# A batched weight gradient with Strassen pairs: two more pairs, another visit order, and banks that start from other products

## The chip, the cores and the metric

The kernel runs on one core of a Trainium2 chip. The metric is the device time of one execution in microseconds. A profile of one execution gives the time of each instruction; its span, from the first to the last instruction, is 1.5 to 1.8 us shorter than the device time.

## The reference

```python
batch, m, k, n = 16, 512, 1024, 768
grad_weight = np.einsum('bmk,bmn->kn', input, grad_output)   # float32
```

With the batch folded into the rows this is one product: X is 8192 x 1024, G is 8192 x 768, and the output X^T G is 1024 x 768 in float32. The contraction runs over 8192 rows, 64 slices of 128.

## The kernel before

**Slices, pairs, quarters.** The 64 slices are loaded as 32 items of two slices. The output is cut in four blocks: A (left half of the columns of X, left half of those of G), B (left, right), C (right, left) and D (right, right), each 512 x 384, that is four quarters of 128 rows. A matmul takes 128 columns of X as weights and 384 columns of G as moving operand. An item of the kind `s` in `LOADS` stays two single slices, each of which adds to A, B, C and D: 16 matmuls a slice, 32 for the two. An item of the kind `P` is a Strassen pair: its two slices are treated as the second index of a 2 x 2 block product, so seven products do the work of eight: 28 matmuls. Two of the seven go straight to A and D; the others are collected in five sums of their own, m, n, o, p and q, and are added to the blocks they belong to once at the end.

**The presums.** A pair needs sums and differences of its bf16 halves. VectorE makes them in six instructions, `sum_g1`, `sum_g2`, `sum_g3` (lines 130, 134, 139), `sum_x1`, `sum_x2`, `sum_x3` (lines 144, 148, 153). Then m = (x2)(g2), n = (x1)(raw g), o = (raw x)(g3), p = (raw x)(g3), q = (x1)(raw g), D takes x3 and g1, A takes x3 and g1.

**Banks.** PSUM has eight banks here, two groups of four (one bank for a quarter). So only two products are open at a time. `ORDER` is a list of visits. `A14:2` brings product A up to its item 14; a figure after the colon says how many of the four banks ScalarE drains (the last ones); a part after `!` closes the product, and its four figures say how many VectorE presums or shares are put in the queue ahead of the drain of each quarter; a figure in front of the letter puts presums ahead of the visit. An engine does its own list in order. A bank that VectorE drains is added to the running sum in SBUF (line 295, or 293 where it is the first). A bank that ScalarE drains has first been filled with the running sum by ScalarE (line 267), so that the matmuls add on to it, and is copied out at the end (line 291). Another product can open a group only when the one before has been drained from its banks.

**Shares.** At the end `SHARES` lists the additions of m to q to the blocks: `t1`, `t2`, `t3` for the upper rows, `l1`, `l2`, `l3` for the lower, each for four quarters. `t1`, `t2`, `l1`, `l2` are 768 columns wide and serve two blocks in one instruction (line 162); `t3` (line 173) and `l3` (line 184) subtract from one block, 384 columns.

**Loads and stores.** The first slice comes in float32 by the queues of SyncE and ScalarE and is rounded by VectorE and ScalarE (`round_by`, line 202). The others are issued by GpSimd and rounded to bf16 on the way, one slice at a time (lines 110 and 112), from item `MERGED` on two slices together (lines 105 and 106). Fourteen items can be held; a load waits for a free buffer. The output is stored by SyncE a quarter at a time, in program order (line 299). The last quarter of the last visit is split in 256 and 128 columns, with a store for each (lines 327 to 336), where the last visit also opens its product.

Of the kernel before, what the change touches and what calls it, by code (L numbers as in the profile page):

```python
# [1 line left out]

# [5 lines left out]

P = 128

LOADS = "ssssssssPPPPPPPPPPPPPPPPPPPPPsss"

ORDER = (
    "A1:4 C1:2!0,0,0,0 D1:2 A2!0,0,0,0 D2 B3:4 D3 D4!0,0,0,0 B4 C4:2 C5 B5 C6!0,0,0,0 B6 A6:2 B7 "
    "A8!0,0,0,0 D8:2 B8 B9 D10!0,0,0,0 B10 B11 C7:2 C9 B12 C11 B13!0,0,0,0 C12 C13 A14:2 C14 "
    "C16!0,0,0,0 A15 B16:2!3,0,0,0 D16:2 3A17!3,0,0,1 n2:4!0,1,1,0 D17 D18 m2:4!3,0,1,0 "
    "q3:4!1,1,1,1 D19 o1:4 o2 o3 1o4!2,1,0,0 D20!0,0,0,0 p4:4 n3:3 3p5!3,0,0,0 n4 A21:2!3,0,0,1 "
    "n6 1m6:4!3,1,0,1 n7 o7:2!2,0,0,1 q7:2!2,0,0,2 n8 p8:2!2,0,0,1 D24:2!1,1,0,2 n9 A25:3!3,0,1,1 "  # L20
    "n10 o10:2!2,0,0,1 m10:2 2n11!2,0,0,1 m11 q11:2!2,0,1,1 p12:2!1,1,0,2 D28:2 m12 3D29!3,0,0,0 "
    "m13 A28:2 2m14!1,0,0,0 A30 o12:2 o13 3o15!3,0,0,1 A31 q15:2!2,1,0,2 A32!0,0,0,0 n16:2 "
    "D32:4!6,1,1,1 p17:2 1n18!3,0,0,0 p18 m17:2 2p19!3,0,0,0 m19 D35:3!3,1,0,2 o20:2 m20 "
    "3o21!2,0,0,0 m21!0,0,0,0 q20:2 p20:4 p21!4,1,0,0 q21!0,0,0,0 D39:0 n21:4!3,1,0,1 D41 "
    "A37:4!2,1,1,1 D42 B17:0 D43!6,0,0,0 B19 B22!0,0,0,0 C19:0 C22!0,0,0,0 A43:0!4,0,0,0 "
).split()


SHARES = (
    "t10 t11 t12 t13 l20 t20 t21 t22 t23 l21 l22 l23 l10 l11 l12 l13 l30 l31 l32 l33 t30 t31 t32 "  # L30
    "t33 "
).split()

WARMUP = [512] * 10 + [128] * 2
PAIRS_HELD = 14
SUMS_HELD = 9

MERGED = 7


@with_exitstack
def kernel(
# [6 lines left out]
    nc = tc.nc  # L49
# [4 lines left out]
    _, _, N = grad_output.shape  # L54
    S = B * M // P
    KH = K // 2
    NH = N // 2
    Q = KH // P
# [3 lines left out]
    OUT = out.rearrange("(ks p) n -> p ks n", p=P)  # L62
# [7 lines left out]
    acc = accp.tile([P, 2 * Q, N], f32, name="acc")  # L70

    macc = accp.tile([P, 5, Q, NH], f32, name="macc")
    SLOT = {"n": 0, "p": 1, "m": 2, "o": 3, "q": 4}
# [23 lines left out]
    items = []  # L97
# [56 lines left out]

    def settled(row, q):
        for p, (_, banks) in opened.items():
            assert p not in ("CD" if row else "AB") or not banks[q][1]

    def share(row, slots, q):
        settled(row, q)  # L160
        dst = acc[:, row + q, :].rearrange("p (h n) -> p h n", h=2)
        nc.vector.tensor_add(out=dst, in0=dst, in1=macc[:, slots, q, :])  # L162

    def top1(q):
        share(0, slice(2, 4), q)

    def top2(q):
        share(0, slice(1, 5, 3), q)

    def top3(q):  # L170
        settled(0, q)
        c = acc[:, q, 0:NH]
        nc.vector.tensor_sub(out=c, in0=c, in1=macc[:, 4, q, :])  # L173

    def low1(q):
        share(Q, slice(0, 3, 2), q)

    def low2(q):
        share(Q, slice(1, 4, 2), q)

    def low3(q):
        settled(Q, q)
        c = acc[:, Q + q, NH:N]
        nc.vector.tensor_sub(out=c, in0=c, in1=macc[:, 0, q, :])

    filler = []
    for i, item in enumerate(items):
        if item[0] == "P":
            filler += [(f, i) for f in (sum_g1, sum_g2, sum_g3, sum_x1, sum_x2, sum_x3)]
    share_by = {"t1": top1, "t2": top2, "t3": top3, "l1": low1, "l2": low2, "l3": low3}  # L190
    filler += [(share_by[c[:2]], int(c[2:])) for c in SHARES]
    filler.reverse()

    def fill(n):
# [20 lines left out]
    streams = {  # L215
        p: [i for i, item in enumerate(items) if item[0] in KINDS.get(p, "P")] for p in "ABCDmnopq"
    }

    LAST_PAIR = max([i for i, item in enumerate(items) if item[0] == "P"], default=0)

    def operands(p, i, q):
        kind, x, g = items[i]
# [16 lines left out]
    def sum_of(p, q):  # L239
        if p in SLOT:  # L240
            return macc[:, SLOT[p], q, :]
        row = q if p in "AB" else Q + q
        return acc[:, row, 0:NH] if p in "AC" else acc[:, row, NH:N]
# [3 lines left out]
    slots = [0, 1]  # L247
    used = set()

    def visit(p, upto, byact, close, ahead, last):  # L250
        items_now = streams[p][done[p] : upto]
        done[p] = upto
        opening = p not in opened
        if opening:

            tail = p in "ABCD" and streams[p][upto - len(items_now)] > LAST_PAIR - 2
            slot = slots.pop(0)
            banks = []
            for q in range(Q):
                name = f"bank{slot * Q + q}"  # L260
                bank = psum.tile([P, 512], f32, name=name)[:, 0:NH]
                act = q >= Q - byact
                carried = act and not fresh[p]
                assert not (carried and tail)
                if carried:
                    assert name in used
                    nc.scalar.copy(out=bank, in_=sum_of(p, q))  # L267
                used.add(name)
                banks.append((bank, carried, act))
            opened[p] = (slot, banks)  # L270
        slot, banks = opened[p]
        final = upto == len(streams[p])

        def mm(q, j):
            stat, mov = operands(p, items_now[j], q)
            bank, carried, _ = banks[q]
            nc.tensor.matmul(  # L277
                bank,
                stat,
                mov,  # L280
                start=opening and j == 0 and not carried,
                stop=close and j == len(items_now) - 1,
                skip_group_check=carried,
            )

        def shut(q):
            fill(ahead[q])
            bank, _, act = banks[q]
            dst = sum_of(p, q)
            if act:  # L290
                nc.scalar.copy(out=dst, in_=bank)  # L291
            elif fresh[p]:
                nc.vector.tensor_copy(out=dst, in_=bank)  # L293
            else:
                nc.vector.tensor_add(out=dst, in0=bank, in1=dst)  # L295
            if final and p in "ABCD":
                row = q if p in "AB" else Q + q
                c0 = 0 if p in "AC" else NH
                nc.sync.dma_start(out=OUT[:, row, c0 : c0 + NH], in_=dst)

        if len(items_now) == 1:
            for q in range(Q):
                mm(q, 0)
            if close:
                for q in range(Q):
                    shut(q)
        else:
            for q in range(Q):
                if last and q == Q - 1 and opening:
                    break  # L310
                for j in range(len(items_now)):
                    mm(q, j)
                if close:
                    shut(q)
            else:
                q = None
            if q is not None:

                fill(ahead[q])
                dst = sum_of(p, q)  # L320
                row = q if p in "AB" else Q + q
                b0 = 0 if p in "AC" else NH
                for c0, c1, name in ((0, 256, None), (256, NH, f"bank{slots[0] * Q}")):
                    bank = banks[q][0] if name is None else psum.tile([P, 512], f32, name=name)
                    for j in range(len(items_now)):
                        stat, mov = operands(p, items_now[j], q)
                        nc.tensor.matmul(
                            bank[:, 0 : c1 - c0],
                            stat,
                            mov[:, c0:c1],  # L330
                            start=j == 0,
                            stop=j == len(items_now) - 1,
                        )
                    d = dst[:, c0:c1]
                    nc.vector.tensor_add(out=d, in0=bank[:, 0 : c1 - c0], in1=d)  # L335
                    nc.sync.dma_start(out=OUT[:, row, b0 + c0 : b0 + c1], in_=d)
        if close:
            fresh[p] = False
            del opened[p]
            slots.append(slot)  # L340

    for n, step in enumerate(ORDER):
        step, _, ahead = step.partition("!")
        step, _, byact = step.partition(":")
        at = next(c for c in step if c.isalpha())
        before, upto = step.split(at)
        if n == 1:
            round_by("DVE", g0, gf, NH, N)
        if n == 2:
            round_by("DVE", x1, xf[1], 4 * P, 6 * P)  # L350
            round_by("ACT", x1, xf[1], 6 * P, 8 * P)
            round_by("DVE", x1, xf[1], 0, 2 * P)
            round_by("ACT", x1, xf[1], 2 * P, 4 * P)
        fill(int(before or 0))
        ahead = [int(a) for a in ahead.split(",")] if ahead else None
        visit(at, int(upto), int(byact or 0), ahead is not None, ahead, n == len(ORDER) - 1)
    assert not filler and not opened


# [28 lines left out]
```

## Time and profile before

| what | value |
|---|---|
| device time, median of three | 166.4 us (166.32 to 166.52) |
| profiled span | 164.9 us |
| TensorE busy, matmuls | 158.8 us, 958 (12 of them a warm-up) |
| VectorE busy, instructions | 114.3 us, 231 |
| ScalarE busy, instructions | 83.1 us, 196 |
| read from HBM, written | 58.72 MB, 3.15 MB |

A share of busy time is a mean over the whole span. What matters for a change of the order is which engine the others wait for in each stretch, which the chain of waits shows. Matmuls overlap: the duration of one, 328 ns, is about twice the step from one start to the next. The loads keep the DMA engines busy to about 141 us, as the page's slices show:

```profile
DMA  5999999999999999999999999999999999300875
```

The three columns after that are without a transfer, and the last belong to the stores.

### The profile page before, as it was taken

What the parts mean: (1) busy time and instruction counts of PE and PEld (TensorE: products, weight loads), DVE (VectorE), ACT (ScalarE), POOL (GpSimd) and SP (SyncE); (2) the same over time, 40 slices, a digit from 0 to 9 for tenths busy, and PEclk for the clock granted to TensorE, in tenths of its full rate; (3) what the DMA queues carried; (4) which work ended last, traced back from release to release, by engine and by line L of the source; (5) the groups of instructions that cost most, each with busy time, mean ns of one, the idle gap of its engine ahead of it and who ended that gap; (6) DMA issues with size and microseconds to landing.
All of it is one profiled execution on the core that took longest, in us unless ns stands there. A gap on an engine that the chain in (4) does not pass through costs nothing.

```text
span 164.9 us, 2645 instructions
## 1 busy us (share of the span) xinstructions
PE 158.8 (96%) x958; PEld 93.8 (57%) x958; DVE 114.3 (69%) x231; ACT 83.1 (50%) x196; POOL 39.9 (24%) x79
## 2 busy tenths in 40 slices
PE   8999999999999999999999999999999999999991
PEld 2456556566545656555566566545656566566560
DVE  0602222002969678879997997998858979999992
ACT  3554442150726586875766744357645568970000
POOL 7444535432222222222222222222122000000000
PEclk9999999999999999999999999999999999999998
DMA  5999999999999999999999999999999999300875
GB/s 179 294 207 208 209 207 210 208 218 209 220 209 216 213 209 218 211 208 221 208 212 213 213 213 214 213 210 215 213 216 212 215 211 214 75 0 0 288 284 191
DMA packets 13836, 33.39 MB, mean 203 GB/s; under 512 B 1536, under 2 KB 5632, under 8 KB 13824
## 3 DMA queue, kind: packets, MB, share of 16 engines
q0 software_dynamic: 10800, 28.64, 89.0%
q1 hardware_dynamic: 2736, 3.54, 6.2%
q10 hardware_dynamic: 288, 1.05, 1.6%
q8 instruction: 7, 0.11, 0.3%
q14 instruction: 5, 0.04, 0.1%
HBM read 58.72 MB, written 3.15 MB: 375 GB/s over the span
## 4 chain that ended last, share of the span: by engine, by line
PE 91%; DVE 6%; issue 1%; DVEq 0%
PE bank L277 88%; PE bank L88 3%; DVE acc L295 3%; DVE xe L144 1%; DVE acc L293 1%; DVE macc L295 1%; DVE acc L173 0%; DVE xp L153 0%; DVE acc L335 0%; DVE xe L148 0%; DVEq L383 0%
## 5 line engine op out<-in xcount | busy, mean ns | idle before, releaser
L277 PEld LDWEIGHTS <-xp 128*128 128x128 bf16 x682 | 66.7, 98 | 46.1 <-issue 1.3
L277 PE MATMUL bank<-gp,xp 128*128 128x384 bf16 x514 | 88.4, 328 | 0.3 <-DVE acc L293 0.2
L291 ACT COPY macc<-bank 128x384 f32<-128x384 f32 x63 | 27.5, 488 | 26.8 <-PE bank L277 26.6
L295 DVE TENSOR_TENSOR acc<-bank,acc 128x384 f32<-128x384 f32 x39 | 19.9, 553 | 28.0 <-PE bank L277 27.7
L291 ACT COPY acc<-bank 128x384 f32<-128x384 f32 x48 | 21.3, 485 | 35.7 <-PE bank L277 35.2
L277 PEld LDWEIGHTS <-xe 128*128 128x128 bf16 x252 | 24.4, 98 | 17.4 <-DVE xe L144 1.5
L277 PE MATMUL bank<-ge,xp 128*128 128x384 bf16 x168 | 31.1, 327 | 0.7 <-DVE xp L153 0.7
L277 PE MATMUL bank<-gp,xe 128*128 128x384 bf16 x168 | 30.4, 327 | 0.6 <-DVE xe L144 0.6
L106 POOL DMA_DIRECT2D xp<-in_input_dram x25 | 13.2, 527 | 41.8 <-DMA xp<-in_input_dram 24.3
L105 POOL DMA_DIRECT2D gp<-in_grad_output_dram x25 | 13.2, 527 | 31.8 <-DMA gp<-in_grad_output_dram 11.4
L295 DVE TENSOR_TENSOR macc<-bank,macc 128x384 f32<-128x384 f32 x29 | 15.2, 554 | 6.6 <-PE bank L277 6.3
L267 ACT COPY bank<-macc 128x384 f32<-128x384 f32 x43 | 19.2, 505 | 0.0
L267 ACT COPY bank<-acc 128x384 f32<-128x384 f32 x36 | 16.1, 497 | 0.0
L144 DVE TENSOR_TENSOR xe<-xp 128x1024 bf16<-128x1024 bf16 x21 | 14.4, 685 | 1.9 <-DMA xp<-in_input_dram 1.9
L277 PE MATMUL bank<-ge,xe 128*128 128x384 bf16 x84 | 15.5, 327 | 0.0
L153 DVE TENSOR_TENSOR xp<-xp 128x1024 bf16<-128x1024 bf16 x21 | 14.4, 685 | 0.0
L162 DVE TENSOR_TENSOR acc<-acc,macc 128x768 f32<-128x768 f32 x16 | 14.1, 953 | 0.0
L130 DVE TENSOR_TENSOR ge<-gp 128x768 bf16<-128x768 bf16 x21 | 11.6, 552 | 0.8 <-DMA gp<-in_grad_output_dram 0.8
L139 DVE TENSOR_TENSOR gp<-gp 128x768 bf16<-128x768 bf16 x21 | 11.6, 552 | 0.0
L148 DVE TENSOR_TENSOR xe<-xp 128x512 bf16<-128x512 bf16 x21 | 8.8, 419 | 0.0
L112 POOL DMA_DIRECT2D xp<-in_input_dram x12 | 6.5, 538 | 9.0 <-DMA xp<-in_input_dram 6.8
L110 POOL DMA_DIRECT2D gp<-in_grad_output_dram x13 | 7.1, 549 | 3.8 <-DMA gp<-in_grad_output_dram 3.1
(18 smaller groups left out, 27.6 us busy)
## 6 DMA issues: line engine op xcount, KB each, us to landing
xp<-in_input_dram POOLq DMA_DIRECT2D x25, 512.0 KB, 16.9
gp<-in_grad_output_dram POOLq DMA_DIRECT2D x25, 384.0 KB, 16.7
xp<-in_input_dram POOLq DMA_DIRECT2D x12, 256.0 KB, 8.5
out_dram<-acc SPq DMA_DIRECT2D x15, 192.0 KB, 2.1
gp<-in_grad_output_dram POOLq DMA_DIRECT2D x13, 192.0 KB, 8.5
xf<-in_input_dram ACTq DMA_DIRECT2D x2, 512.0 KB, 4.9
gf<-in_grad_output_dram SPq DMA_DIRECT2D x2, 192.0 KB, 4.4
out_dram<-acc SPq DMA_DIRECT2D x1, 128.0 KB, 1.9
```

The lines of the kernel that those rows point to most:

```text
L105: nc.gpsimd.dma_start(out=gp, in_=G[rows, :].rearrange("(p m) n -> p m n", m=2))
L106: nc.gpsimd.dma_start(out=xp, in_=X[rows, :].rearrange("(p m) k -> p m k", m=2))
L130: nc.vector.tensor_add(out=ge[:, 0:2, :], in0=g[:, :, 0, :], in1=g[:, :, 1, :])
L139: nc.vector.tensor_sub(out=g[:, 1:3, :], in0=g[:, 1:3, :], in1=g[:, 3::-3, :])
L144: nc.vector.tensor_add(out=xe[:, 0:2, :].rearrange("p a k -> p (a k)"), in0=xp[:, 0, :], in1=xp[:, 1, :])
L148: nc.vector.tensor_add(out=extra[i][0][:, 2, :], in0=xp[:, 0, 0:KH], in1=xp[:, 1, KH:K])
L153: nc.vector.tensor_sub(out=x[:, 1:3, :], in0=x[:, 1:3, :], in1=x[:, 0::3, :])
L162: nc.vector.tensor_add(out=dst, in0=dst, in1=macc[:, slots, q, :])
L267: nc.scalar.copy(out=bank, in_=sum_of(p, q))
L277: nc.tensor.matmul(bank, stat, mov, start=opening and j == 0 and not carried, stop=close and j == len(items_now) - 1, skip_group_check=car ...
L291: nc.scalar.copy(out=dst, in_=bank)
L295: nc.vector.tensor_add(out=dst, in0=bank, in1=dst)
```

## The change

Seven items of single slices in front instead of eight, two at the end instead of three: 23 pairs instead of 21. Loads are merged from item 2 instead of 7. `ORDER` and `SHARES` are new. A visit may now carry a sign and a letter: `A39:0-q` has ScalarE fill the four banks of A with minus the sum q before the visit, and `D37:0+m` those of D with m, so that the shares of q in A (`t3`) fall away and those of m in D shrink to the other block. The banks of C's last visit are filled by ScalarE from C's own sum and copied out by it, which the kernel before did not allow so late. The two stores of a split last quarter go by two queues where there is such a split. The purpose is fewer matmuls and less work for VectorE at the end.

```diff
-LOADS = "ssssssssPPPPPPPPPPPPPPPPPPPPPsss"
+LOADS = "sssssssPPPPPPPPPPPPPPPPPPPPPPPss"
...
-    "A1:4 C1:2!0,0,0,0 D1:2 A2!0,0,0,0 D2 B3:4 D3 D4!0,0,0,0 B4 C4:2 C5 B5 C6!0,0,0,0 B6 A6:2 B7 "
...
-    "3o21!2,0,0,0 m21!0,0,0,0 q20:2 p20:4 p21!4,1,0,0 q21!0,0,0,0 D39:0 n21:4!3,1,0,1 D41 "
-    "A37:4!2,1,1,1 D42 B17:0 D43!6,0,0,0 B19 B22!0,0,0,0 C19:0 C22!0,0,0,0 A43:0!4,0,0,0 "
+    "C1:2!0,0,0,0 B1:1 D2!0,0,0,0 B2 A3:2!0,0,0,0 D4:1!0,0,0,0 B4!0,0,0,0 C4 B6:2!0,0,0,0 "
+    "A6!0,0,0,0 C6!0,0,0,0 B8:4!0,0,0,0 D8 D10!0,0,0,0 C10:3 A8:2 A10!0,0,0,0 C11 C12 B12:4 "
+    "C14!0,0,1,0 B14!2,0,0,0 A14:2 3A15 D15:4!3,0,2,1 n2:4!1,2,0,0 A16!0,0,0,0 m2:4 1q3:4!2,1,1,1 "
...
+    "p16:3!3,0,1,1 o17!0,0,0,0 D29:3 m15:1 m17 6m18!4,0,0,0 D32 n18:4!2,1,1,1 D33!1,0,0,0 q18 q19 "
+    "A30:4 1q20!5,0,0,0 A33!0,0,0,1 p19 n21:4!5,0,1,1 o22:1!1,1,1,1 p22 p23!3,0,0,0 o23:4!0,0,0,0 "
+    "m21 q23:4!3,0,1,0 m23!1,0,0,0 A39:0-q n23:4!4,0,0,1 A41!1,0,0,0 D37:0+m B18:1!3,1,0,1 "
+    "D41!4,0,0,0 C15:4 C18!0,0,0,0 "
...
-    "t10 t11 t12 t13 l20 t20 t21 t22 t23 l21 l22 l23 l10 l11 l12 l13 l30 l31 l32 l33 t30 t31 t32 "
-    "t33 "
+    "l20 l21 l22 t20 t21 t10 t11 t12 t13 t22 t23 l10 l11 l12 l13 l23 l30 l31 l32 l33 "
...
-MERGED = 7
+MERGED = 2
...
+        sides = [
+            (h, p)
+            for h, p in enumerate((left, right))
+            if p and ("ABCD"[(row > 0) * 2 + h], p) not in taken
+        ]
...
-            tail = p in "ABCD" and streams[p][upto - len(items_now)] > LAST_PAIR - 2
...
-                assert not (carried and tail)
...
+                elif first:
+                    assert name in used and not fresh[p] and not byact
+                    src = macc[:, SLOT[first[1]], q, :]
+                    if first[0] == "-":
+                        nc.scalar.mul(out=bank, in_=src, mul=-1.0)
+                    else:
+                        nc.scalar.copy(out=bank, in_=src)
...
-                    nc.sync.dma_start(out=OUT[:, row, b0 + c0 : b0 + c1], in_=d)
+                    store = nc.scalar if name is None else nc.sync
+                    store.dma_start(out=OUT[:, row, b0 + c0 : b0 + c1], in_=d)
...
+    rounded = False
...
-        if n == 2:
+        if not rounded and done[at] < 2 <= int(upto):
+            rounded = True
             round_by("DVE", x1, xf[1], 4 * P, 6 * P)
```

## The prediction

> **What bounds the kernel now.** I read the page first, then the chain of waits in order of time, then the timeline of the last 15 us and the table by stretches. The page:
>
> ```profile
> PE 158.8 (96%) x958; PEld 93.8 (57%) x958; DVE 114.3 (69%) x231; ACT 83.1 (50%) x196; POOL 39.9 (24%) x79
> ...
> PE 91%; DVE 6%; issue 1%; DVEq 0%
> ```
>
> TensorE is busy nearly throughout, so its matmuls are the first suspect. The chain in order of time says where it is not:
>
> ```profile
> 7.97 39.99 PE bank L277 x245
> ...
> 49.00 0.61 DVE xe L144
> ...
> 49.65 59.30 PE bank L277 x363
> ...
> 110.94 0.61 DVE xp L153
> ...
> 111.60 44.23 PE bank L277 x271
> ...
> 155.84 2.02 DVE acc L295 x4
> ```
>
> Three long runs of matmuls, broken at 49 and 111 us by VectorE work that makes operands of pairs, and from 155.8 us on VectorE alone up to the stores. The end, in the timeline:
>
> ```profile
> 149.79 10.40 PE L277 MATMUL bank<-gp,xp 128*128 128x384 bf16 x63
> ...
> 151.94 5.93 DVE L295 TENSOR_TENSOR acc<-bank,acc 128x384 f32<-128x384 f32 x12
> 152.52 9.01 SPq L299 DMA_DIRECT2D out_dram<-acc  x15
> 157.78 1.95 DVE L173 TENSOR_TENSOR acc<-acc,macc 128x384 f32<-128x384 f32 x4
> 159.66 1.48 DVE L295 TENSOR_TENSOR acc<-bank,acc 128x384 f32<-128x384 f32 x3
> ...
> 161.05 0.61 DVE L335 TENSOR_TENSOR acc<-bank,acc 128x256 f32<-128x256 f32 x2
> 161.62 0.90 SPq L336 DMA_DIRECT2D out_dram<-acc  x2
> ```
>
> The reader is to see two rates. 63 matmuls in 10.40 us are (10.40 - 0.327)/62 = 0.1625 us each. And VectorE has no hole: 12 adds, 4 shares, 3 adds follow one another, and SyncE issues a store about every 0.46 us. The stretches confirm it (PE, PEld, DVE, ACT, POOL):
>
> ```profile
> 44.30:141.00 96.70, 95.42 (x586) 56.82 (x584) 82.85 (x171) 59.56 (x142) 20.04 (x38) 1.00 1.07 213
> 141.00:161.20 20.20, 20.18 (x131) 12.35 (x128) 20.10 (x35) 6.47 (x15) 0.00 (x0) 1.00 0.37 125
> ```
>
> From 44 to 141 us VectorE is busy 86%; in the last 20 us, 20.10 of 20.20. So the end has two bounds side by side, TensorE and VectorE. TensorE's account: the first product starts at 5.21, 934 x 0.1625 plus six halves of 0.109 and six of 0.055 is 152.8, the last ends at 161.18, so some 3.0 us are lost: 1.3 before 7.97 (nine matmuls in 2.76 us instead of 1.46), 0.74 at 49.65, 0.12 at 75.6, 0.87 at 111.60.
>
> **What the Trainium skill says.** "TensorE: Matmul & The Clock Gate", section "Wait — 56ns, not 53.3ns?", has start to start at N/2.4 GHz + 2.5 ns warm and N/1.2 GHz cold: 162.5 and 320 ns for 384 columns. The trace agrees: 0.1625 above, and the first four products start 0.32 apart. "VectorE: DVE Perf Modes", section "The perf-mode tier table", gives tensor_tensor two elements a cycle in bf16 and one in fp32 or from PSUM; the trace agrees (768 columns: 552 ns in bf16, 953 in fp32). "ScalarE: Activation LUTs", section "What ACT_TABLE_LOAD costs", prices an ACTIVATE with immediates at 186 + 0.833 N ns, 506 here, overlapping 93 back to back; the bank copies of line 267 measure 497 to 505.
>
> **The change, part by part.** Counts come from walking both orders through `visit`; for the kernel before they equal the page's.
>
> *Matmuls.* Nine single pairs and 23 Strassen pairs: A and D have 41 items each, B and C 18, m to q 23 each, times four quarters: 932, against 940. The last step C18 finds its group already open (C15 opened it), so the split of the last quarter is not used, nor the new store queue with it. 932 x 0.1625 = 151.45: 1.3 us less than 152.8.
>
> *VectorE.* Back-to-back steps, start to start, from the timelines: x sums 0.60, 0.335, 0.60; g sums 0.47, 0.27, 0.47 (2.74 us a pair, though durations add to 3.25); an add or copy from a bank 0.474; a 768-wide share 0.869 ((2.69 - 0.953)/2 for three at 136.10); a 384-wide one 0.469. Two pairs more: +5.5. Adds and copies from banks, 104 against 72: +15.2 (many early, where VectorE idles). Wide shares 12 against 16: -3.5. Narrow shares 8 in both. Less the two halves of L335, 0.6: +16.6 us in all. From step n2 (44 us) to the end of q23 (140 us) I sum 88.6 us of steps in 95.6, 93% against 86: tighter, but every presum I followed to its matmul, by these sums and the landings, arrives in time, often by only 0.1 to 0.2 us.
>
> *ScalarE.* Copies out 116 against 111, bank copies 101 against 79, eight of them with another product (-q for A, +m for D): 0.37 x 5 + 0.413 x 22 = 11 us more on an engine half idle. The multiply by -1 has no row; I take 0.5 us, between 0.485 (copy out) and 0.506 (the skill's price). A39's and D37's banks are filled behind a 24-matmul and an 8-matmul step: hidden. What this buys is the loss of four narrow shares (t3) and the halving of four wide ones (l1): 4 x 0.469 + 4 x 0.40 = 3.5 us of VectorE at the end.
>
> *Opening.* C1 reads columns 512 on, which are rounded last (about 5.4 us instead of 5.2), and the right half of G is rounded behind two copies of C1's banks, to about 7.3. I get eight products by 8.0 where before had nine by 7.97: +0.2 us. D4's fourth bank, refilled by ScalarE after A3's copy: +0.15.
>
> *Loads.* Merged loads were issued 4.31 us apart a pair (91.33, 95.65, 99.94), single ones 2.2 a slice (16.53, 18.69). Five pairs more merged: about 0.45 us earlier. But merging makes a slice wait for its partner. Slice 3's x lands at 11.83; 4.31 a pair from there puts pair 2 at 16.15, needed at 16.7, and pair 4 at 24.75, or 25.65 if the late landing of before recurs (its issue gap of 1.64 us at 24.01 against 0.7 elsewhere), needed by D10 at 25.1: 0 to 0.5 us of wait.
>
> *Total for TensorE*: 5.21 + 1.3 + 0.2 + 0.15 + 0.25 (middle of 0 to 0.5) + 151.45 = 158.6, and 0.1 to 0.5 for the tight presums.
>
> *The end.* Here is what I think decides. The last Strassen pair is now load pair 29, not 28. Its x load was issued at 117.43 and landed 16.7 later, 134.15; now 133.7. Its x sums end at 135.3, then VectorE has four adds of p23 (which also need p23's matmuls: 135.2 plus the waits above), and without a hole: 12 wide shares (10.43), 8 narrow (3.75) and the adds of m23, A41, B18 and D41, with p23's 19 in all: 18 x 0.474 and 0.55 for the last. Sum 23.3. From p23's first add at 135.4 D41's last so ends at 158.7, at about TensorE's end and 2.7 us after D41's own matmuls (16 matmuls before that end). C18 is drained by ScalarE by 159.3, but its four stores stand behind D41's in SyncE's one queue: D41's last issue at 158.8, C18's last four steps of 0.465 later, 160.65; landing 2.2 (1.9 to 2.4 in the row of twelve stores), and 1.1 from the last landing to the end, as now (163.77 to 164.87). Span 164.0, against 164.87: 0.9 us less, of which TensorE's saving is only partly paid out. With the 1.6 us between span and time: **165.6**.
>
> **Rivals.** *TensorE sets the end.* If VectorE were early, the last copy out ends 0.7 after TensorE's 158.4, lands 2.0 later, plus 1.1: span 162.2, time 163.8; with part of the queue 164.2. For it: the order gives the closings of q, n, o to ScalarE (byact 4). Against: the sum of VectorE above leaves it no slack after 135 us. *New waits eat the gain.* 0.7 us more of tight presums or of the queue: 166.3. For it: margins of 0.1 to 0.2 us in series, an engine at 93%. *A wait takes the place of the waits removed.* Pair 4 late by 0.5, then pairs 8 to 11 and VectorE's backlog cost TensorE a microsecond or more as at 111 us (0.87), all passed on to p23's adds and the end: +1.6, 167.2. For it: VectorE has 16.6 us more to do and the last pair comes 4.3 us later. Against: singles in front leave TensorE fed to 40 us.
>
> **Chances.** Forecast 0.50 (165.6), TensorE's end 0.15 (164.2), gain eaten 0.16 (166.3), wait in its place 0.19 (167.2). Faster than 166.07: 0.66; within 0.2%: 0.15; slower: 0.19. The range leaves out half of the TensorE case and some 0.08 above: 164.8 to 167.1.
>
> **What would show it.** 932 product matmuls; no hole in VectorE from about 134 to 158 us; D41's stores over 2 us after its matmuls; SyncE issuing the last eight stores 0.46 apart with ScalarE's last copy done over a microsecond before the last issue; TensorE's gaps under 1 us after 9 us. Wrong if the last store follows ScalarE's copy at once, if matmuls wait for operands by 1 us or more, or if pair 4's load holds D10 by over 0.5 us.

## The result, and the profile after

The changed kernel takes 166.97 us (median of four runs, 166.90 to 167.21), the kernel before 166.46; the ratio is 1.0032 with a 95% interval of 1.0014 to 1.0049. It became slightly slower. Beside the later runs the kernel before took 166.62 to 166.65, so that a difference of two medians below is uncertain by some 0.2 us; each ratio is to the kernel before as measured beside that run. Yet TensorE did finish earlier. The page of the kernel after:

```profile
PE 156.8 (95%) x944; PEld 92.3 (56%) x944; DVE 130.4 (79%) x269; ACT 95.8 (58%) x223; POOL 34.7 (21%) x69
...
PE 79%; DMA 14%; ACT 2%; issue 1%; POOL 1%; ACTq 0%; POOLq 0%
```

944 matmuls are 12 of the warm-up and the 932 that were counted; VectorE has 16.1 us more (16.6 was forecast), ScalarE 12.7 more (11 was forecast). The chain of waits in order of time (start, duration, what):

```profile
9.90 15.70 DMA xp<-in_input_dram
...
25.65 13.19 PE bank L285 x80
...
40.19 117.78 PE bank L285 x723
...
159.51 0.48 ACT acc L299
```

The two breaks at 49 and 111 us are gone: one run of matmuls from 40 to 158 us. In their place stands a wait for a load at 25.65. Read by itself the chain says that matmuls and then ScalarE's copies set the end, for it closes with L299. That is where one can be misled: it follows instructions, and the last copy ends at 159.99, 5.1 us before the span does. The timeline of the end shows what is left out (start, duration, engine, line, what):

```profile
136.18 1.95 DVE L303 TENSOR_TENSOR macc<-bank,macc 128x384 f32<-128x384 f32 x4 [0.33 <-PE bank L285]
...
150.03 11.66 SPq L307 DMA_DIRECT2D out_dram<-acc  x16
...
151.46 7.96 PE L285 MATMUL bank<-gp,xp 128*128 128x384 bf16 x48
...
157.33 1.94 DVE L303 TENSOR_TENSOR acc<-bank,acc 128x384 f32<-128x384 f32 x4
158.05 1.94 ACT L299 COPY acc<-bank 128x384 f32<-128x384 f32 x4 [1.64 <-PE bank L285]
```

The first line is p23's four adds, the fourth D41's, the fifth C18's copies. TensorE ends at 151.46 + 7.96 = 159.42, 1.8 us earlier than before (161.18). SyncE's row ends at 161.69: its last issue comes 1.3 us after the last copy. And between the first and the fourth line VectorE has no hole, in the table by stretches (PE, PEld, DVE, ACT, POOL):

```profile
44.30:136.10 91.80, 91.80 (x566) 55.10 (x565) 84.66 (x181) 57.51 (x135) 20.06 (x38) 1.00 1.07 213
...
136.18:159.27 23.09, 23.09 (x143) 13.74 (x141) 23.09 (x39) 15.24 (x38) 0.00 (x0) 1.00 0.44 122
```

23.09 of 23.09 us. TensorE is fully busy as well, so shares can't decide which of the two sets the end; that was put to runs. D41's four products were complete before 157 us (C's last 16 matmuls follow them, 16 x 0.1625 = 2.6 us), but its adds end at 159.27. Then eight stores land one after another from 159.77 to 163.97, where the kernel before had twelve stores gone by 160.29 and five left, two of them parts. What these eight stores are doing, the stretches tell (after the five engines: granted clock, busy share of the DMA engines, GB/s):

```profile
158.80:161.60 2.80, 0.62 (x4) 0.17 (x2) 0.47 (x2) 1.17 (x3) 0.00 (x0) 1.00 1.03 363
161.60:163.10 1.50, 0.00 (x0) 0.00 (x0) 0.00 (x0) 0.00 (x0) 0.00 (x0) 0.53 0.99 359
163.10:163.70 0.60, 0.00 (x0) 0.00 (x0) 0.00 (x0) 0.00 (x0) 0.00 (x0) 0.50 0.05 18
```

The DMA engines are full to 163.1 us, at about 360 GB/s, and then only a trickle of the last stores is left, for 0.6 us.

### The profile page after: what moved, and what is told of

It is laid out like the page before. It is cut to its first block, busy times and chain, and to the rows that moved or that the text cites. A ratio compares the mean times of both kernels' runs of the same rounds, so it can differ in the third digit from the quotient of the medians.

```text
span 165.1 us, 2713 instructions
## 1 busy us (share of the span) xinstructions
PE 156.8 (95%) x944; PEld 92.3 (56%) x944; DVE 130.4 (79%) x269; ACT 95.8 (58%) x223; POOL 34.7 (21%) x69
## 4 chain that ended last, share of the span: by engine, by line
PE 79%; DMA 14%; ACT 2%; issue 1%; POOL 1%; ACTq 0%; POOLq 0%
PE bank L285 79%; DMA xp<-in_input_dram 14%; ACT acc L299 1%; POOL gp L111 1%; ACT bank L266 0%; ACTq L299 0%; POOLq L385 0%
## 5 line engine op out<-in xcount | busy, mean ns | idle before, releaser
L285 PE MATMUL bank<-gp,xp 128*128 128x384 bf16 x472 | 81.1, 326 | 1.9 <-DVE gp L206 0.9
L299 ACT COPY macc<-bank 128x384 f32<-128x384 f32 x71 | 31.1, 488 | 28.1 <-PE bank L285 28.0
L303 DVE TENSOR_TENSOR acc<-bank,acc 128x384 f32<-128x384 f32 x52 | 26.1, 550 | 17.6 <-PE bank L285 17.6
L299 ACT COPY acc<-bank 128x384 f32<-128x384 f32 x45 | 20.1, 489 | 24.7 <-PE bank L285 24.6
L107 POOL DMA_DIRECT2D xp<-in_input_dram x30 | 15.9, 530 | 51.5 <-DMA xp<-in_input_dram 26.3
L266 ACT COPY bank<-macc 128x384 f32<-128x384 f32 x53 | 23.6, 491 | 2.8 <-DVE acc L303 2.1
L106 POOL DMA_DIRECT2D gp<-in_grad_output_dram x30 | 16.0, 532 | 38.9 <-DMA gp<-in_grad_output_dram 20.1
L303 DVE TENSOR_TENSOR macc<-bank,macc 128x384 f32<-128x384 f32 x39 | 19.8, 548 | 2.2 <-PE bank L285 2.0
L189 DVE TENSOR_TENSOR acc<-acc,macc 128x768 f32<-128x768 f32 (+1 forms) x20 | 14.6, 787 | 0.0
L135 DVE TENSOR_TENSOR ge<-gp 128x384 bf16<-128x384 bf16 x23 | 8.0, 348 | 0.0
L301 DVE COPY acc<-bank 128x384 f32<-128x384 f32 x11 | 5.5, 551 | 1.4 <-PE bank L285 1.4
```

Of the source, the lines that this page charges most:

```text
L106: nc.gpsimd.dma_start(out=gp, in_=G[rows, :].rearrange("(p m) n -> p m n", m=2))
L107: nc.gpsimd.dma_start(out=xp, in_=X[rows, :].rearrange("(p m) k -> p m k", m=2))
L189: op(out=dst, in0=dst, in1=src)
L285: nc.tensor.matmul(bank, stat, mov, start=opening and j == 0 and not carried, stop=close and j == len(items_now) - 1, skip_group_check=car ...
```

## The experiments

Two theories: **(1)** from p23's first add on, VectorE's unbroken work sets the time of D41's adds, and C's stores come behind D's; TensorE matters only through the moment at which p23 is complete. **(2)** What the page's chain says: matmuls, then C18's copies.

**B18 drained by ScalarE.**

```diff
-    "m21 q23:4!3,0,1,0 m23!1,0,0,0 A39:0-q n23:4!4,0,0,1 A41!1,0,0,0 D37:0+m B18:1!3,1,0,1 "
+    "m21 q23:4!3,0,1,0 m23!1,0,0,0 A39:0-q n23:4!4,0,0,1 A41!1,0,0,0 D37:0+m B18:4!3,1,0,1 "
```

> The changed kernel (166.97 us) with one figure of its order edited: B's last visit is drained by ScalarE in all four quarters (B18:4 in place of B18:1), so VectorE has three adds, 1.4 us, less between p23's adds and D41's last add. Theory 1 (VectorE's unbroken work after p23 and then SyncE's queue of stores set the end): D41's last add ends about 1.4 us earlier, C's stores no longer queue behind D41's, the last store follows ScalarE's last copy; 165.1 to 165.7 us. Theory 2 (the page's chain: matmuls, then ScalarE's copies of C18 set the end): no change, 166.9 to 167.1.

165.60 us; against the kernel before 0.9943 (0.9930 to 0.9955). One figure of the order makes 1.4 us, and the kernel is faster than the one before. Its timeline:

```profile
150.15 10.38 SPq L307 DMA_DIRECT2D out_dram<-acc  x16
...
156.17 1.94 DVE L303 TENSOR_TENSOR acc<-bank,acc 128x384 f32<-128x384 f32 x4
158.17 1.94 ACT L299 COPY acc<-bank 128x384 f32<-128x384 f32 x4 [1.64 <-PE bank L285]
```

D41's adds now end at 158.11, and SyncE's row ends at 160.53, just behind ScalarE's last copy (160.11). TensorE and the copies came no earlier than in the changed kernel (158.17 against 158.05 for the first copy), so theory 2 can't account for the gain. Not all of it is the three adds, though. The last store is issued 1.15 us earlier (160.14 against 161.29), and it lands 2.22 us after its issue instead of 2.68: the other 0.46 us belong to the landings, to which the last part comes back.

**Twelve matmuls fewer after p23.** The last three pairs of A39 are left out, so A is incomplete.

```diff
         def mm(q, j):
+            if p == "A" and upto == 39 and j >= 3:
+                return
```

> The changed kernel, leaving out 12 matmuls of A's visit A39 (the products of its last three pairs, so A is incomplete): TensorE has 1.95 us less to do after p23 and the other engines the same. Theory 1 (VectorE and the store queue): no change, 166.8 to 167.1 us. Theory 2 (matmuls and then C18's copies set the end): 1.9 us less, about 165.1.

166.88 us, ratio 1.0015 (1.0008 to 1.0022): of the 1.95 us taken from TensorE the time shows 0.1 in the median, 0.3 in the ratio. The timeline:

```profile
156.79 1.94 ACT L301 COPY acc<-bank 128x384 f32<-128x384 f32 x4 [0.95 <-PE bank L287]
157.06 1.94 DVE L305 TENSOR_TENSOR acc<-bank,acc 128x384 f32<-128x384 f32 x4
157.30 4.04 SPq L309 DMA_DIRECT2D out_dram<-acc  x8
```

ScalarE's copies end at 158.73, 1.26 us earlier than in the changed kernel and before D41's adds (159.00), and SyncE still issues to 161.3. Theory 2 falls.

**Without the banks that start from q and m.**

```diff
-    "m21 q23:4!3,0,1,0 m23!1,0,0,0 A39:0-q n23:4!4,0,0,1 A41!1,0,0,0 D37:0+m B18:1!3,1,0,1 "
+    "m21 q23:4!3,0,1,0 m23!1,0,0,0 A39:0 n23:4!4,0,0,1 A41!5,0,0,0 D37:0 B18:1!3,1,0,1 "
...
-    "l20 l21 l22 t20 t21 t10 t11 t12 t13 t22 t23 l10 l11 l12 l13 l23 l30 l31 l32 l33 "
+    "l20 l21 l22 t20 t21 t10 t11 t12 t13 t22 t23 t30 t31 t32 t33 l10 l11 l12 l13 l23 l30 l31 l32 l33 "
```

> The changed kernel without the banks that start from another product: A39 and D37 open as usual, q is subtracted from A by four shares (t3) and the shares l1 are 768 wide again. VectorE has 4 x 0.469 + 4 x 0.40 = 3.5 us more after p23. Theory 1 (VectorE's work after p23 sets the end): 3.2 to 3.5 us more, 170.2 to 170.5. Theory 2 (matmuls set the end): under 1 us more, below 168.

170.48 us, ratio 1.0223 (1.0202 to 1.0244), 3.5 us more. The profiled execution took 171.71: it opened with cold matmuls (0.32 us from one to the next in place of 0.1625) to 10.9 us, so the stretch is what to read:

```profile
137.49:164.05 26.56, 23.84 (x143) 13.74 (x141) 26.56 (x43) 13.24 (x31) 0.00 (x0) 1.00 0.35 102
```

From p23's first add to D41's last: 26.56 us without a hole, against 23.09, 3.47 more, where 3.5 was summed. So filling the banks from other products is worth what it takes off VectorE here, one for one.

**D's stores from GpSimd.**

```diff
-                nc.sync.dma_start(out=OUT[:, row, c0 : c0 + NH], in_=dst)
+                store = nc.gpsimd if p == "D" else nc.sync
+                store.dma_start(out=OUT[:, row, c0 : c0 + NH], in_=dst)
```

> The changed kernel, with D's four stores issued by GpSimd in place of SyncE; nothing else differs. Theory 1: C's four stores no longer stand behind D41's, the last issue falls from 161.3 us to about 160.0, just behind ScalarE's last copy; 1.2 to 1.8 us less, 165.2 to 165.8, unless GpSimd's own stores take over 1 us longer to land than SyncE's. Theory 2 (matmuls and copies set the end, the queue costs nothing): 166.9 to 167.1.

170.13 us, ratio 1.0212 (1.0198 to 1.0226): 3.2 us slower, and both theories missed it; theory 1 had named slow landings from GpSimd as its exception. Its page has the issues:

```profile
out_dram<-acc SPq DMA_DIRECT2D x12, 192.0 KB, 2.0
...
out_dram<-acc POOLq DMA_DIRECT2D x4, 192.0 KB, 3.3
```

SyncE issued its last store at 160.04, as hoped, but it landed 4.86 us later, at 164.90: the eight landings stretch from 160.38 to 164.90, though the issues end earlier. And from the last landing to the end of the span there are 3.3 us instead of 1.2, which is 2.1 of the 3.2 us. That points away from SyncE's issues as the limit of the eight stores, but half of them now came from another engine and queue; the next run asks with SyncE alone.

**C's stores in pairs.**

```diff
+                if p != "C":
                     nc.sync.dma_start(out=OUT[:, row, c0 : c0 + NH], in_=dst)
+                elif q % 2:
+                    nc.sync.dma_start(
+                        out=OUT[:, row - 1 : row + 1, c0 : c0 + NH],
+                        in_=acc[:, row - 1 : row + 1, c0 : c0 + NH],
+                    )
```

> The changed kernel with C's last visit stored in two DMAs of two quarters each in place of four: SyncE issues six stores instead of eight after D41's first add, the bytes stay the same. Theory A (SyncE's rate of issue, one in 0.46 to 0.5 us, sets the last store): the last issue falls from 161.3 to about 160.3, about 1.0 us less, 165.9 to 166.1. Theory B (the transfers of the eight quarters set it, which landed 0.53 us apart): the landings from D41's first, 159.8, plus seven times 0.53 stay at 163.5; 0 to 0.5 us less, 166.5 to 167.0.

167.28 us, ratio 1.0040 (1.0026 to 1.0054), above both ranges, though the interval overlaps that of the changed kernel. The issues of this run:

```profile
157.94 1.80 SPq L308 DMA_DIRECT2D out_dram<-acc  x4
159.84 0.95 SPq L310 DMA_DIRECT2D out_dram<-acc  x2
```

The last is issued at 160.34, the 1.0 us earlier that was asked for, and lands at 164.06, no earlier than the 163.97 of the changed kernel. Theory A falls: not SyncE's rate but the transfers hold the last eight quarters, as the full DMA engines of the changed kernel have it too. They count from D41's first store, which VectorE times. One landing is late here too: the first 384 KB took 1.71 us after the landing ahead of it, the second 0.91.

**Eight matmuls of C ahead of D10.**

```diff
-    "A6!0,0,0,0 C6!0,0,0,0 B8:4!0,0,0,0 D8 D10!0,0,0,0 C10:3 A8:2 A10!0,0,0,0 C11 C12 B12:4 "
+    "A6!0,0,0,0 C6!0,0,0,0 B8:4!0,0,0,0 D8 C8:3 D10!0,0,0,0 C10 A8:2 A10!0,0,0,0 C11 C12 B12:4 "
```

> The changed kernel with eight matmuls of C (its items 6 and 7, already landed) put between D8 and D10, so that TensorE works while pair 4 lands. D10's wait of 0.68 us goes. Theory 1 (waits of TensorE before p23 shift p23's adds and with them VectorE's unbroken stretch and the end): 0.4 to 0.6 us less, 166.3 to 166.6. Rival (the time is given back at the next tight operand, or at the x load of pair 29): within 0.1 us of 166.97.

166.39 us, ratio 0.9988 (0.9981 to 0.9995): 0.6 us less, and D10 no longer waits. The profiled execution took 166.78, as its first product came 0.4 us later than in the changed kernel (5.84 against 5.44). What TensorE loses at 25 us is still missing at the end; from there to p23 it has no slack to make it good.

**Loads of items 2 to 6 single again.**

```diff
-MERGED = 2
+MERGED = 7
```

> The changed kernel with the loads of items 2 to 6 one slice at a time again (MERGED = 7). Theory A (D10's wait of 0.68 us for the load of pair 4 comes from merging, as the prediction's step has it): the wait goes, TensorE runs 0.7 us earlier, 0.4 to 0.6 us less, 166.4 to 166.6. Theory B (it comes from the late landing near 22 to 24 us and from the order, since slice 9 landed at 25.77 us unmerged too): the wait stays at 0.5 to 0.8 us and the pairs land 0.2 to 0.5 us later; 166.9 to 167.3.

167.18 us, ratio 1.0028 (1.0017 to 1.0040): no gain. The waits of TensorE's weight loads in this run, and in the changed kernel:

```profile
PEld L285 <- DMA xp<-in_input_dram: 1.3, 2, 1.0
```

```profile
PEld L285 <- DMA xp<-in_input_dram: 1.1, 2, 0.9
```

Theory B: single loads make D10 wait as long (1.0 against 0.9 us for the longest). Merging neither caused the wait nor brought anything that the time shows.

**The kernel before with C's last visit on ScalarE.**

```diff
-    "A37:4!2,1,1,1 D42 B17:0 D43!6,0,0,0 B19 B22!0,0,0,0 C19:0 C22!0,0,0,0 A43:0!4,0,0,0 "
+    "A37:4!2,1,1,1 D42 B17:0 D43!6,0,0,0 B19 B22!0,0,0,0 C19:4 C22!0,0,0,0 A43:0!4,0,0,0 "
...
-                assert not (carried and tail)
```

> The kernel before with one part of the change alone: C's last visit is filled and drained by ScalarE in all four quarters (C19:4), four adds less for VectorE in the last 10 us. Theory 1 (at the end VectorE sets the time in the kernel before as well, until the last quarter's halves): the four shares t3 and A's first adds come 1.9 us earlier, A's stores no longer stack up before the last one, whose issue at 162.1 us falls to 161.7; 0.3 to 0.5 us less, 165.9 to 166.1. Theory 2 (matmuls set it): no change within 0.2%.

166.18 us, ratio 0.9970 (0.9959 to 0.9981): 0.4 us less, the gain that theory 1 has, though the interval just reaches the 0.2% of theory 2. This part of the change alone helps the old kernel:

```profile
155.47 1.95 DVE L173 TENSOR_TENSOR acc<-acc,macc 128x384 f32<-128x384 f32 x4
...
158.09 0.56 DVE L294 TENSOR_TENSOR acc<-bank,acc 128x384 f32<-128x384 f32 x1 [0.67 <-PE bank L276]
```

The shares t3 come 2.3 us earlier than the 157.78 of before, of which some 0.2 are the execution's (TensorE is that much earlier at 111.4 us already, ahead of the edit). And VectorE now waits for TensorE: the bound changed hands.

**Both edits, and the opening.** First C ahead of D10 together with B18 on ScalarE.

> Both edits: eight matmuls of C ahead of D10, and B18 drained by ScalarE. With VectorE's end 1.4 us earlier, the last store follows ScalarE's copies, and they follow TensorE, which is 0.6 us earlier than with B18 alone (165.6). Theory 1: 164.9 to 165.2. If VectorE's adds of D41 or SyncE's queue still hold the end: 165.3 to 165.6.

164.84 us, ratio 0.9884 (0.9869 to 0.9899): the two gains add up, 1.2% below the kernel before and just under the range of theory 1. Then, on top, C1's banks on ScalarE and the second half of G rounded first:

```diff
-    "C1:2!0,0,0,0 B1:1 D2!0,0,0,0 B2 A3:2!0,0,0,0 D4:1!0,0,0,0 B4!0,0,0,0 C4 B6:2!0,0,0,0 "
+    "C1:4!0,0,0,0 B1:1 D2!0,0,0,0 B2 A3:2!0,0,0,0 D4:1!0,0,0,0 B4!0,0,0,0 C4 B6:2!0,0,0,0 "
...
-        if n == 1:
+        if n == 0:
             round_by("DVE", g0, gf, NH, N)
```

> Beside the two edits that gave 164.84 us (C ahead of D10, B18 by ScalarE), the opening: C1's four banks are drained by ScalarE and the right half of the first slice of G is rounded ahead of them, so that B1 no longer waits behind two copies of VectorE. B1 starts at about 6.7 us in place of 7.2 to 7.3. Theory 1 (whatever TensorE gains before p23 reaches the end): 0.3 to 0.5 us less, 164.3 to 164.6. Rival (D2 or the x load of the last pair takes it back): 164.7 to 165.0.

164.57 us, ratio 0.9875 (0.9861 to 0.9888). The median is 0.3 us lower, but the intervals overlap. B1 starts 0.7 us earlier, yet in the profile TensorE is no earlier at 148 us (148.38 against 148.34): waits at 11.9 us for a load and at 48.5 us for an operand, 0.5 us and 0.3, take it back, as the rival has it. Whether this edit is worth anything stays open.

## Why the prediction was wrong

It forecast 165.6 us and faster; 166.97 lies inside its range, 164.8 to 167.1, on the other side of no change. Point by point:

- **The mechanism of the end was right.** VectorE's unbroken stretch after p23 was summed to 23.3 us and measured 23.09; the run with three adds fewer and the one with four shares more and four wider changed that stretch by about what they took and gave (1.27 us where 1.42 was summed, 3.47 where 3.48 was). TensorE's loss of 12 matmuls there moved the time hardly at all.
- **The step that failed is the moment of p23's first add.** It was set at 135.4 and came at 136.18. The prediction's 135.2 for p23's matmuls comes out as its 7.11 us of start, opening and waits plus 788 x 0.1625; TensorE was through these 788 at 135.81. Allowed were 0.15 us of wait for D4 and 0.25 for D10 (the middle of 0 to 0.5), and 0.1 to 0.5 for tight presums. Measured: D4's bank 0.23, D10 0.68 (the load of pair 4 landed at 25.60, D10 was ready at 24.96), A14's third bank, filled behind ScalarE's copies, 0.24 at 40.19, where nothing was allowed; the presums were in time but for three waits of 0.05. Over 0.5 us at D10 was the prediction's own sign of being wrong. The late landing near 23 us was in the trace of before and was taken at half its weight; the run with eight matmuls ahead of D10 returned 0.6 us.
- **The same step put a lag at nothing.** The last matmul of p23's first quarter starts at 135.65 and ends at 135.98, and VectorE, idle since 135.85, starts its add at 136.18, so that 0.36 us pass after TensorE's 788 steps. Of the 0.8 us about half is that TensorE came later than allowed, and half is this lag. D41's last add so ended at 159.27 instead of 158.7.
- **The second is the eight stores.** They were priced at 0.465 for each issue, with SyncE's rate as the limit, and 2.2 us for the last landing. The row of twelve stores in the trace of before had it otherwise: issued 0.488 apart on the mean (152.52 to 157.89), landed 0.534 apart (154.42 to 160.29). With B18 on ScalarE eight landings are 0.533 apart (158.63 to 162.36), the last 2.22 after its issue, and pairing the stores left the end where it was: the limit is the transfer. As long as the landings are even, the two ways of pricing give nearly the same end. In the changed kernel they are not even, and the last takes 2.68: two of the steps are 0.82 and 0.84. A fetch of instructions of 8 KB stands at 161.68 in its trace. In every trace here with B18:1 in the order such a fetch stands among the last eight stores (159.9 to 163.8), and a landing is late there; in the three with B18:4 it stands at 155 to 156, and the last eight landings are even. So some 0.5 us of what B18:4 gains may be where the fetch falls. That the fetch is the reason was not tried.
- **The sum.** D41's last add 0.57 late, the issues 0.07, the last landing 0.48: 1.1 us over the 164.0 of the span, which is 165.1. The rest is 1.8 instead of 1.6 us between span and time.
- **Smaller steps.** The opening did not cost 0.2 us: B1 began at 7.15, so eight products were out by 7.8. VectorE's tighter middle stretch held: it was busy for 84.66 of 91.80 us, 92%, where 93% was summed. Merging was said to gain 0.45 us of landing at the price of a wait; the last pair's x did land 0.5 earlier (133.69 against 134.15), but TensorE was later than that, and the wait is there without merging. The multiply by -1 takes as long as a copy (1.73 us for four).
- **The rivals.** "TensorE sets the end" would need VectorE early; even with B18 on ScalarE the end still counts from D41's adds or the copies. "A wait takes the place of the waits removed" named pair 4 and is in part what happened, without the backlog of VectorE that it added: the 1.73 us of waits at 49, 76 and 111 us before became 1.3 after the opening.

Where the expected gain went: TensorE's end, 1.8 us earlier, did not reach the output. D41's products waited behind the shares in VectorE's list, and four more quarters had to follow them through the same transfer.

## What to carry to other kernels

When two engines are full at the end, take work from each in turn by a small edit and see which moves the time; busy shares and a chain that ends on the wrong engine don't tell. Follow the chain past the last instruction: if the last store is issued later than its data are ready, the true predecessor is the work that the stores ahead of it waited for. And stores cost their transfer, here 0.53 us for each 192 KB: spread them, and let the engine with room drain whatever sits just ahead of the last block. Where an add waits for a matmul, count the lag from the last step of TensorE to the add, here 0.36 us.

## What was not expected of the hardware

- Four stores of 192 KB issued by GpSimd at the end landed 2.2 to 4.8 us after issue, where SyncE's took 1.9 to 2.1 for the same four in the changed kernel, and the span ended 3.3 us after the last landing instead of 1.2. Why it ends so late was not asked.
- Two stores of 384 KB land no sooner than four of 192 KB issued up to 1 us later (164.06 against 163.97).
- The cold start of TensorE differs between executions of the same opening: most of the profiles here show 0.1625 us from one matmul to the next from about 7 us on, the profiled execution without seeded banks 0.32 us up to 10.9 us.
